# Sample attention of a hybrid decoder step: even and odd cache rows in the two column halves, and TensorE's order pinned by phases

## The chip, the cores and the metric

One core of one Trainium2 chip runs the whole kernel. The metric is device time in microseconds of one execution, the median of several runs; smaller is better.

## What is computed

One decoder layer for 256 prompt tokens and for 64 sample tokens (8 sequences with 8 new tokens each). The part that matters here is the attention of the sample tokens. Each sequence has 1024 rows of a compressed cache (512 latent values and 64 rotary values per row), which lie in 8 pages named by a page table. 8 heads attend from each of the 8 new tokens to these 1024 rows and, causally, to the 8 new rows of their own sequence:

```python
def mla_sample_attention(q_lat, q_pe, ckv_new, kpe_new, cache_ckv_l, cache_kpe_l, page_table):
    ckv_past = cache_ckv_l[page_table].reshape(Bd, -1, KV_RANK)
    kpe_past = cache_kpe_l[page_table].reshape(Bd, -1, ROPE_DIM)
    s_past = einsum('bthc,bsc->bhts', q_lat, ckv_past) + einsum('bthr,bsr->bhts', q_pe, kpe_past)
    s_new = einsum('bthc,bsc->bhts', q_lat, ckv_new) + einsum('bthr,bsr->bhts', q_pe, kpe_new)
    s_new = where(causal, s_new, -inf)
    p = softmax(concatenate([s_past, s_new], axis=-1) * MLA_SCALE, axis=-1)
    return (einsum('bhts,bsc->bthc', p[..., :P], ckv_past)
            + einsum('bhts,bsc->bthc', p[..., P:], ckv_new))
```

All of it is in 32-bit floats.

## The kernel before

The kernel is written for a framework that orders the instructions of each engine itself, from the order of the program and its own estimate of times, and that places every wait. Weights stream through three buffers `raw` of 1 MB (pool `wraw`); ScalarE and VectorE split them into a high and a low part (`whi`, `wlo`, pool `whl`, three of each), and TensorE multiplies each block three times (`mm3`). PSUM has four banks named `acc` and four named `aux`.

The sample attention stands between two projections that are put into its neighbourhood on purpose: `early_proj(0)` ahead of it, together with the last scores and values of the prompt attention, and `early_proj(1)` behind it, into which `sample_tail` lays the rest of the last sequence. It loops over the 8 sequences b. For each:

- `gather` (L738) fetches the 1024 cache rows by three indirect DMAs on GpSimd's queue: the rotary rows `kraw`, and the latent rows in two halves of 1 MB, the first into `craw` (pool `sr`, 3 buffers), the second into a `raw` buffer. Partition p holds 8 consecutive rows.
- `past_scores` (L755) is called once for each half. TensorE turns four 128x128 blocks at a time into one bank of `aux` (`transpose`, L134); ScalarE and VectorE in turn copy the bank to `th`. The queries `qst` (64 columns: 8 heads by 8 tokens) are the weights and `th` the moving operand. The 64 columns fill one half of the array, so two matmuls are issued for the two halves: half 0 adds up latent blocks 0 and 2, half 1 blocks 1 and 3, of the same 512 cache rows. `fold` (L731) adds the two halves: ScalarE copies partitions 64 to 127 of the bank down, VectorE adds. The sum is written to `Ss`, 64 partitions by 1088 columns.
- `new_scores` (L786) does the same for the 64 new rows of all sequences, with a mask (`C_NEW`) that leaves the sequence's own.
- `softmax` (L794) works on `Ss`, 64 partitions by 1088 columns, with the division at its end.
- `turn` (L802) turns the probabilities (eight blocks of 64x128 and one of 64x64), `values` (L812) multiplies them with the cache rows (eight matmuls with 512 columns, even ones in half 0, odd ones in half 1) and with the new rows `ckvs`, and `latent` (L822) adds the two halves by a matmul with a folding matrix and turns the result to `olat`.

The work of sequence b - 1 (`turn`, `values`) and of b - 2 (`latent`) is put between the steps of sequence b by the table `at`. What order TensorE gets in the end is the framework's choice. A matmul in 32-bit floats is two instructions in the profile (two LDWEIGHTS and two MATMUL), a transpose is one.

Of the kernel before, what the change touches and what calls it, by code (L numbers as in the profile page):

```python
# [18 lines left out]
NP = 256  # L19
NB = 8  # L20
# [18 lines left out]
C_NEW, C_VM, C_PEXP, C_PR, C_SEL, C_END = 1408, 1920, 1924, 2052, 2053, 2181  # L39


def _consts():
# [23 lines left out]
    for b in range(NB):  # L66
        ok = (r[None, :] // NT == b) & (r[None, :] % NT <= r[:, None] % NT)
        c[:NS, C_NEW + b * NS:C_NEW + (b + 1) * NS] = np.where(ok, 0.0, -1e30)
# [14 lines left out]
def tile_hgrn2_mla_step(  # L83
# [45 lines left out]

    def mm(out, lhsT, rhs, start, stop):  # L130
        nc.tensor.matmul(out, lhsT=lhsT, rhs=rhs, start=start, stop=stop)  # L131

    def transpose(out, in_, k):
        nc.tensor.transpose(out=out, in_=in_, identity=ident[:k, :k])  # L134
# [588 lines left out]
    with pool("sr", 3) as sr, pool("sc", 2) as sc, pool("s1") as s1:  # L723
# [31 lines left out]
        def past_scores(b, hf, S, kraw, craw, at):  # L755
            psc = bank(acc)
            ths = []

            def scores(f):
                for g in range(2):  # L760
                    mm(psc[64 * g:64 * (g + 1)], qst[:, f + g, b], ths[f + g], f == 0, False)

            for f in range(RF):
                pt = bank()
                for j in range(4):
                    transpose(pt[:, j * P:(j + 1) * P], craw[:, j, f * P:(f + 1) * P], P)
                th = sc.tile([P, 512], F32, name="th", bufs=4)
                cp(f, th, pt)
                ths.append(th)
                if f == 2:  # L770
                    scores(0)
                if f in at:
                    at[f]()
            pt = bank()
            for j in range(2):
                transpose(pt[:, j * P:(j + 1) * P],
                          kraw[:, 4 * hf + 2 * j:4 * hf + 2 * j + 2].rearrange("p o c -> p (o c)"), P)
            kt = sc.tile([P, 2, P], F32, name="ktp")
            cp(hf, kt, pt[:, 0:256].rearrange("p (j s) -> p j s", j=2))
            scores(2)  # L780
            pv_ = psc.rearrange("p (j o s) -> p o j s", j=2, o=2)
            for g in range(2):
                mm(pv_[64 * g:64 * (g + 1), g], qst[:, 4 + g, b], kt, False, True)
            fold(S, psc, slice(hf * 512, (hf + 1) * 512), 512)

        def new_scores(b, S):  # L786
            psn = bank(acc)
            for f in range(RF):
                g = f % 2
                mm(psn[64 * g:64 * (g + 1), 0:NS], qst[:, f, b], ckvT[:, f, NP:N], f < 2, f == 3)  # L790
            mm(psn[0:64, 0:NS], qst[:, 4, b], kpeT[:, NP:N], False, True)
            fold(S, psn, slice(PAST, PAST + NS), NS, cst[0:NS, C_NEW + b * NS:C_NEW + (b + 1) * NS])

        def softmax(S):  # L794
            mx = sc.tile([NS, 2], F32, name="mxs")
            nc.vector.tensor_reduce(out=mx[:, 0:1], in_=S, axis=AX.X, op=ALU.max)
            nc.vector.tensor_scalar(out=mx[:, 0:1], in0=mx[:, 0:1], scalar1=-SCALE, scalar2=None, op0=ALU.mult)
            nc.scalar.activation(out=S, in_=S, func=AF.Exp, scale=SCALE, bias=mx[:, 0:1], accum_out=mx[:, 1:2])
            nc.vector.reciprocal(out=mx[:, 1:2], in_=mx[:, 1:2])
            nc.vector.tensor_scalar(out=S, in0=S, scalar1=mx[:, 1:2], scalar2=None, op0=ALU.mult)  # L800

        def turn(S):  # L802
            pt, pt2 = bank(), bank()
            for j in range(8):
                transpose(pt[:, j * 64:(j + 1) * 64], S[:, j * P:(j + 1) * P], 64)
            transpose(pt2[0:64, 0:64], S[:, PAST:PAST + NS], 64)
            PT = sc.tile([P, 9, 64], F32, name="PTs")
            nc.scalar.copy(out=PT[:, 0:8], in_=pt.rearrange("p (j t) -> p j t", j=8))
            nc.vector.tensor_copy(out=PT[0:64, 8], in_=pt2[0:64, 0:64])
            return PT  # L810

        def values(PT, craws):  # L812
            po = bank(acc)
            for j in range(8):
                g = j % 2
                mm(po[64 * g:64 * (g + 1)], PT[:, j], craws[j // 4][:, j % 4], j < 2, j == 7)
            mm(po[0:64], PT[0:64, 8], ckvs, False, True)
# [586 lines left out]
```

## Time and profile before

| | us |
|---|---|
| median of 3 runs | 2173.68 (2171.99 to 2177.36) |
| the profiled execution, its own time | 2173.57 |
| its span, first to last instruction | 2171.5 |
| TensorE busy in the span | 2120.1 (98%) |
| VectorE busy | 1079.2 (50%) |
| ScalarE busy | 878.0 (40%) |
| GpSimd busy | 168.0 (8%) |

TensorE is busy almost all the time; the other engines work beside it. The mean granted TensorE clock is 0.993 of full speed. The sample attention lies between about 362 and 524 us of the span. Matmuls overlap, so their busy times add up to more than the time that they take; where the cost of a matmul is wanted, the distance between the starts of two weight loads (engine PEld) tells more.

### The profile page before, as it was taken

The page shows a single profiled execution, that of the slowest core. Times are in us where ns is not written, and L with a number is a line of the kernel's source. Part 1 is how long each engine was busy: PE and PEld are TensorE (multiplying, and loading weights), DVE is VectorE, ACT ScalarE, POOL GpSimd, SP SyncE. Part 2 cuts the span into 40 slices and gives each one's busy share as a digit, 9 for nine tenths or more (in the row PEclk, how much of TensorE's full clock was granted, in tenths as well). Part 3 has the DMA queues.
Part 4 walks back from the last instruction along what each step waited for, and adds up shares of the span by engine and source line. Part 5 has one row for each costly group of instructions (what it writes and reads, how often), then busy time and mean ns, then how long its engine had stood idle before and what let it go on. Part 6 is the DMA issues. An engine that isn't in the chain of part 4 may idle for free.

```text
span 2171.5 us, 34878 instructions
## 1 busy us (share of the span) xinstructions
PE 2120.1 (98%) x14716; PEld 1907.7 (88%) x14716; DVE 1079.2 (50%) x1648; ACT 878.0 (40%) x1328; POOL 168.0 (8%) x166
## 2 busy tenths in 40 slices
PE   6999999999999999999999899999999999999997
PEld 4788988457788889999999599999999999999996
DVE  3556754444865655533443643444444444444455
ACT  4332443334554444333343543434343333333353
POOL 0000001110432211000011000000000000000001
PEclk9999999999999999999999999999999999999998
DMA  8886455335567777766764555544444454454442
GB/s 255 319 301 238 152 190 197 111 128 160 185 215 240 232 241 253 241 208 204 252 213 141 196 177 168 173 144 148 155 150 144 153 155 142 150 156 148 145 151 71
DMA packets 327572, 401.94 MB, mean 185 GB/s; under 512 B 10985, under 2 KB 265529, under 8 KB 324473
## 3 DMA queue, kind: packets, MB, share of 16 engines
q1 hardware_dynamic: 301576, 363.07, 51.8%
q0 software_dynamic: 3584, 21.50, 2.8%
q10 hardware_dynamic: 22256, 15.16, 2.3%
q8 instruction: 115, 1.88, 0.4%
q14 instruction: 41, 0.33, 0.0%
HBM read 387.69 MB, written 12.01 MB: 184 GB/s over the span
## 4 chain that ended last, share of the span: by engine, by line
PE 92%; DVE 4%; ACT 1%; DMA 1%; issue 1%; POOL 0%; SPq 0%; DVEq 0%; ACTq 0%; POOLq 0%
PE acc L131 79%; PE aux L131 8%; PE aux L134 5%; DMA raw<-in_w_in_dram 1%; DVE wlo L143 1%; ACT whi L146 1%; DVE zu L1367 0%; DVE x L1284 0%; DVE X L143 0%; POOL qt L137 0%; DMA xt<-in_x_prompt_dram 0%; DVE zg L137 0%; DVE qn L494 0%; DVE bb L917 0%; POOL X L137 0%
## 5 line engine op out<-in xcount | busy, mean ns | idle before, releaser
L143 DVE TENSOR_TENSOR wlo<-raw,whi 128x1024 fp32r<-128x1024 f32 (+1 forms) x493 | 602.9, 1228 | 714.3 <-ACT whi L146 709.1
L146 ACT CAST whi<-raw 128x1024 fp32r<-128x1024 f32 (+1 forms) x493 | 502.1, 1025 | 807.6 <-PE acc L131 653.7
L131 PE MATMUL acc<-hh,whi 128*128 128x320 f32 x1168 | 369.8, 317 | 3.7 <-ACT hh L146 2.3
L131 PE MATMUL acc<-hl,whi 128*128 128x320 f32 x1168 | 362.6, 311 | 0.3 <-DVE hl L143 0.3
L131 PE MATMUL acc<-hh,wlo 128*128 128x320 f32 x1168 | 361.5, 311 | 0.0
L131 PE MATMUL acc<-uh,whi 128*128 128x320 f32 x1024 | 316.7, 309 | 0.0
L131 PE MATMUL acc<-gh,whi 128*128 128x320 f32 x1024 | 316.2, 309 | 0.0
L131 PE MATMUL acc<-gh,wlo 128*128 128x320 f32 x1024 | 316.1, 309 | 0.0
L131 PE MATMUL acc<-ul,whi 128*128 128x320 f32 x1024 | 316.1, 309 | 0.0
L131 PE MATMUL acc<-uh,wlo 128*128 128x320 f32 x1024 | 316.1, 309 | 0.0
L131 PE MATMUL acc<-gl,whi 128*128 128x320 f32 x1024 | 315.9, 309 | 0.0
L131 PEld LDWEIGHTS acc<-hh,whi 128*128 128x128 f32 x1168 | 220.2, 189 | 34.2 <-issue 17.5
L131 PEld LDWEIGHTS acc<-hl,whi 128*128 128x128 f32 x1168 | 220.5, 189 | 2.9 <-DVE hl L143 1.4
L131 PEld LDWEIGHTS acc<-hh,wlo 128*128 128x128 f32 x1168 | 219.6, 189 | 3.1 <-DVE wlo L143 2.5
L131 PEld LDWEIGHTS acc<-uh,whi 128*128 128x128 f32 x1024 | 192.5, 188 | 1.7 <-ACT u L1336 0.8
L131 PEld LDWEIGHTS acc<-gh,whi 128*128 128x128 f32 x1024 | 191.9, 187 | 1.8 <-ACT u L1337 0.8
L131 PEld LDWEIGHTS acc<-ul,whi 128*128 128x128 f32 x1024 | 192.4, 188 | 0.0
L131 PEld LDWEIGHTS acc<-uh,wlo 128*128 128x128 f32 x1024 | 192.4, 188 | 0.0
L131 PEld LDWEIGHTS acc<-gh,wlo 128*128 128x128 f32 x1024 | 192.0, 187 | 0.1
L131 PEld LDWEIGHTS acc<-gl,whi 128*128 128x128 f32 x1024 | 192.0, 188 | 0.0
L131 PE MATMUL aux<-raw,cT 128*32 128x512 f32 (+1 forms) x832 | 113.7, 593 | 16.1 <-DVE tt L137 11.2
L140 POOL TENSOR_TENSOR ssum<-ssum,sqt 128x320 f32<-128x320 f32 x26 | 25.9, 997 | 981.2 <-ACT sqt L1217 980.3
(411 smaller groups left out, 2602.7 us busy)
## 6 DMA issues: line engine op xcount, KB each, us to landing
raw<-in_w_ada_dram SPq DMA_DIRECT2D x96, 1024.0 KB, 6.9
raw<-in_w_up_dram SPq DMA_DIRECT2D x64, 1024.0 KB, 5.7
raw<-in_w_down_dram SPq DMA_DIRECT2D x64, 1024.0 KB, 5.8
raw<-in_w_in_dram SPq DMA_DIRECT2D x60, 1024.0 KB, 5.8
raw<-in_w_o_dram SPq DMA_DIRECT2D x16, 1024.0 KB, 5.8
raw<-in_w_in_dram SPq DMA_DIRECT2D x20, 512.0 KB, 6.4
raw<-in_w_b_out_dram SPq DMA_DIRECT2D x8, 1024.0 KB, 6.2
raw<-in_w_a_out_dram SPq DMA_DIRECT2D x8, 1024.0 KB, 5.8
```

The costliest lines, as they stand in the source:

```text
L131: nc.tensor.matmul(out, lhsT=lhsT, rhs=rhs, start=start, stop=stop)
L134: nc.tensor.transpose(out=out, in_=in_, identity=ident[:k, :k])
L140: (eng or nc.vector).tensor_tensor(out=out, in0=a, in1=b, op=ALU.add)
L143: return (eng or nc.vector).tensor_tensor(out=out, in0=a, in1=b, op=ALU.subtract)
L146: nc.scalar.copy(out=hi, in_=src)
```

## The change

The two column halves no longer split the latent blocks of the same rows; half 0 holds the even cache rows of a sequence and half 1 the odd ones. All 1024 scores of a sequence then stand in one bank of 128 partitions by 512 columns, with nothing to fold.

- `turn_keys` turns one latent block of all 1024 rows into two banks (g = 0: even, g = 1: odd) and copies them to the two halves of one buffer from the pool `whl`, which the attention did not use before. `turn_rotary` turns the rotary rows into one bank, which serves both halves. `scores` multiplies; a sequence now has 10 matmuls with 512 columns (five pairs).
- `softmax` reads the bank itself: VectorE takes the maximum over 512 columns on 128 partitions, `swapped` exchanges the halves of a column, and the exponential goes from the bank to `Ss` with the sum beside it. The division is put off: the reciprocal `wgt` is applied as ScalarE copies the values' result from its bank.
- `turn` turns four blocks of 128x128; `values` has the eight matmuls with the cache rows alone.
- The scores of the new tokens (`new_scores`) are made once ahead of the loop, each sequence against its own 8 rows (40 matmuls with 8 columns). Their exponentials `pnew` are kept. In `sample_tail` they are scaled, turned once, spread over a block structure (`pown`, 64 by 512), multiplied with `ckvs` in four matmuls of 512 columns, and added to `olat`.
- `behind` puts every TensorE instruction of a `with` block behind the last one before it. Each sequence has four phases: three latent blocks turned, and `latent` of b - 2; scores of blocks 0 and 1; `turn` of b - 1, block 3 and the rotary rows turned; `values` of b - 1 and the scores of blocks 2, 3 and rotary.
- Pool `sr` has 5 buffers in place of 3, and three of eight half gathers go into `raw` in place of four. Constants shrink by 496 columns.

```diff
+    pe_last = [None]
+    def behind():
+        return tc.issue_after(pe_last[0].ins)
...
-        def fold(S, psc, cs, n, mask=None):
-            S2 = s1.tile([NS, 512], F32, name="Ss2")
-            nc.scalar.copy(out=S2[:, 0:n], in_=psc[64:P, 0:n])
-            if mask is not None:
-                add(S2[:, 0:n], S2[:, 0:n], mask)
-            add(S[:, cs], psc[0:64, 0:n], S2[:, 0:n])
...
-                if hf:
+                if (2 * b + hf) % 8 in (1, 3, 5):
                     craw = wraw.tile([P, 2048], F32, name="raw").rearrange("p (j c) -> p j c", c=RANK)
...
+        def new_scores():
+            psn = bank(acc)
+            for b in range(NB):
+                us, vs = slice(b * NT, (b + 1) * NT), slice(NP + b * NT, NP + (b + 1) * NT)
+                for f in range(RF):
+                    mm(psn[0:NS, us], qst[:, f, b], ckvT[:, f, vs], f == 0, False)
+                mm(psn[0:NS, us], qst[:, 4, b], kpeT[:, vs], False, True)
...
+        def turn_keys(ths, craws, f):
+            pair = whl.tile([P, 1024], F32, name="wlo" if f % 2 else "whi")
+            for g in range(2):
+                pt = bank()
+                for j in range(4):
+                    transpose(pt[:, j * P:(j + 1) * P], craws[j // 2][:, 2 * j % 4 + g, f * P:(f + 1) * P], P)
+                th = pair[:, 512 * g:512 * (g + 1)]
+                cp(f + g, th, pt)
+                ths[f, g] = th
...
+        def scores(b, psc, ths, f):
             for g in range(2):
+                mm(psc[64 * g:64 * (g + 1)], qst[:, f if f < RF else RF + g, b], ths.pop((f, g)), f == 0, f == RF)
...
+        def softmax(b, psc):
+            mx = sc.tile([P, 6], F32, name="mxs")
+            nc.vector.tensor_reduce(out=mx[:, 0:1], in_=psc, axis=AX.X, op=ALU.max)
+            swapped(mx[:, 1:2], mx[:, 0:1])
...
+            nc.scalar.activation(out=S, in_=psc, func=AF.Exp, scale=SCALE, bias=mx[:, 2:3], accum_out=mx[:, 3:4])
+            nc.scalar.activation(out=pnew[:, b], in_=snew[:, b], func=AF.Exp, scale=SCALE, bias=mx[0:NS, 2:3],
+                                 accum_out=lnew[0:NS, b:b + 1])
...
+            nc.vector.reciprocal(out=wgt[:, b:b + 1], in_=mx[:, 5:6])
...
-            mm(po[0:64], PT[0:64, 8], ckvs, False, True)
...
+            nc.scalar.activation(out=ot, in_=po, func=AF.Copy, scale=wgt[:, b:b + 1])
...
         for b in range(NB):
             kraw, craws = gather(b)
+            ths, psc = {}, bank(acc)
+            for f in range(3):
+                turn_keys(ths, craws, f)
+            if done:
+                latent(b - 2, done)
+            with behind():
+                scores(b, psc, ths, 0)
+                scores(b, psc, ths, 1)
+            with behind():
+                if prev:
+                    PT = turn(prev[0])
+                turn_keys(ths, craws, 3)
+                turn_rotary(ths, kraw)
+            with behind():
+                if prev:
+                    done = values(b - 1, PT, prev[1])
+                for f in range(2, 5):
+                    scores(b, psc, ths, f)
+                S = softmax(b, psc)
+            prev = S, craws
...
+            for f in range(RF):
+                pn = bank()
+                mm(pn, ckvs[:, f * P:(f + 1) * P], pown.rearrange("s b q -> s (b q)"), True, True)
+                ov = olat[:, f].rearrange("p h (b t) -> p b h t", t=NT)
+                add(ov, ov, pn.rearrange("p (b h t) -> p b h t", b=NB, h=NH))
```

How the change moves the instructions shows at three places. The first is TensorE's queue in the middle of the loop, before: twelve rows of about twenty-five that make one sequence (`th` are turned keys, `qst` queries, `PTs` turned probabilities; "x4" is four instructions of the program in a row).

```order
L134 MATMUL aux<-ident,Ss 128x64 x8
L134 MATMUL aux<-ident,Ss 64x64
L131 MATMUL acc<-th,qst 64x512
L134 MATMUL aux<-ident,raw 128x128 x4
L131 MATMUL acc<-th,qst 64x512
L134 MATMUL aux<-ident,raw 128x128 x4
L131 MATMUL acc<-craw,PTs 64x512 x4
L131 MATMUL acc<-raw,PTs 64x512 x4
L131 MATMUL acc<-ckvs,PTs 64x512
L134 MATMUL aux<-ident,kraw 128x128 x2
L131 MATMUL acc<-th,qst 64x512 x2
L131 MATMUL acc<-ktp,qst 64x2x128 x2
```

The same queue now, one whole sequence (a sequence whose two halves both lie in `craw`; the keys are now named `whi` and `wlo`):

```order
L139 MATMUL aux<-ident,craw 128x128 x24
L136 MATMUL aux<-cst,ot 128x64 x4
L136 MATMUL acc<-whi,qst 64x512 x2
L136 MATMUL acc<-wlo,qst 64x512 x2
L139 MATMUL aux<-ident,Ss 128x128 x4
L139 MATMUL aux<-ident,craw 128x128 x8
L139 MATMUL aux<-ident,kraw 128x128 x4
L136 MATMUL acc<-craw,PTs 64x512 x4
L136 MATMUL acc<-raw,PTs 64x512 x4
L136 MATMUL acc<-whi,qst 64x512 x2
L136 MATMUL acc<-wlo,qst 64x512 x2
L136 MATMUL acc<-ktp,qst 64x512 x2
```

The matmuls on half the columns stood in six places of a sequence, some alone; now they stand in two blocks of two and seven pairs. The second place is VectorE's queue around a softmax, before:

```order
L140 TENSOR_TENSOR Ss<-acc,Ss_4268 64x512
L727 COPY th<-aux 128x512
L796 TENSOR_REDUCE mxs<-Ss 64x1
L826 COPY olat<-aux 128x32x8
L797 TENSOR_SCALAR mxs<-mxs 64x1
L727 COPY th<-aux 128x512
L799 RECIPROCAL mxs<-mxs 64x1
L800 TENSOR_SCALAR Ss<-Ss,mxs 64x1088
```

And now:

```order
L804 TENSOR_REDUCE mxs<-acc 128x1
L798 COPY mxs<-mxs 64x1
L799 COPY mxs<-mxs 64x1
L732 COPY whi<-aux 128x512
L806 SCALAR_TENSOR_TENSOR mxs<-mxs,mnew 128x1
L732 COPY wlo<-aux 128x512
L808 TENSOR_SCALAR mxs<-mxs 128x1
L732 COPY whi<-aux 128x512
L840 COPY olat<-aux 128x32x8
L145 TENSOR_TENSOR mxs<-mxs,lnew 128x1
```

The wide additions and the wide scaling are gone, and small steps stand between the three key copies of the next sequence. The third place is TensorE's queue ahead of the loop, before (`Sp`, `PTp` and `vv` belong to the last prompt heads):

```order
L134 MATMUL aux<-ident,Sp 128x128 x3
L131 MATMUL aux<-PTp,vv 128x128 x3
L134 MATMUL aux<-ident,Sp 128x128 x3
L131 MATMUL aux<-PTp,vv 128x128 x3
L134 MATMUL aux<-ident,craw 128x128 x12
```

And now, around the second transposes of `Sp`:

```order
L136 MATMUL acc<-ckvT,qst 64x8 x4
L136 MATMUL acc<-kpeT,qst 64x8
L136 MATMUL acc<-ckvT,qst 64x8 x3
L136 MATMUL aux<-PTp,vv 128x128 x3
L139 MATMUL aux<-ident,Sp 128x128 x3
L136 MATMUL acc<-ckvT,qst 64x8
L136 MATMUL acc<-kpeT,qst 64x8
```

Before, the transposes of `Sp` and the matmuls on `PTp` followed each other directly, and the first `craw` came behind them; now 23 and 17 of the 40 small matmuls stand in between.

## Rows read from the trace of the kernel before

**Rows 1.** The page's chain that ended last, shares of the span by engine.

```profile
PE 92%; DVE 4%; ACT 1%; DMA 1%; issue 1%; POOL 0%; SPq 0%; DVEq 0%; ACTq 0%; POOLq 0%
```

**Rows 2.** Windows: loop middle, start, tail; us, busy per engine (instructions), clock, DMA share, GB/s.

```profile
395.67:501.18 105.51, 105.51 (x631) 54.08 (x631) 47.16 (x93) 41.57 (x75) 13.19 (x14) 1.00 0.39 131
362.06:395.67 33.61, 30.91 (x178) 15.98 (x176) 11.56 (x23) 11.10 (x22) 2.19 (x3) 1.00 0.28 105
501.18:524.47 23.29, 23.29 (x150) 18.35 (x150) 7.83 (x13) 6.67 (x10) 0.00 (x0) 1.00 0.48 136
```

**Rows 3.** Timeline of weight loads, one sequence: start us, us, instruction, idle before.

```profile
415.18 0.86 PEld L134 LDWEIGHTS aux<-ident,craw 128*128 128x128 f32 x8 [0.38 <-issue]
416.00 0.97 PEld L131 LDWEIGHTS aux<-cst,ot 128*128 128x128 f32 x8
416.84 0.48 PEld L134 LDWEIGHTS aux<-ident,craw 128*128 128x128 f32 x4
417.49 0.20 PEld L131 LDWEIGHTS acc<-th,qst 128*64 128x64 f32 x4 [0.17 <-issue]
418.50 0.42 PEld L134 LDWEIGHTS aux<-ident,craw 128*128 128x128 f32 x4 [0.81 <-issue]
...
419.30 0.19 PEld L131 LDWEIGHTS acc<-th,qst 128*64 128x64 f32 x2 [0.17 <-issue]
...
421.60 0.86 PEld L134 LDWEIGHTS aux<-ident,raw 128*128 128x128 f32 x8
422.62 0.60 PEld L134 LDWEIGHTS aux<-ident,Ss 64*128 64x128 f32 x9 [0.17 <-issue]
423.32 0.19 PEld L131 LDWEIGHTS acc<-th,qst 128*64 128x64 f32 x2
424.32 0.42 PEld L134 LDWEIGHTS aux<-ident,raw 128*128 128x128 f32 x4 [0.81 <-DVE Ss L140]
...
426.49 0.20 PEld L131 LDWEIGHTS acc<-craw,PTs 128*64 128x64 f32 x4 [0.17 <-issue]
...
430.08 0.19 PEld L131 LDWEIGHTS acc<-ckvs,PTs 64*64 64x64 f32 x2 [0.81 <-issue]
431.08 0.20 PEld L134 LDWEIGHTS aux<-ident,kraw 128*128 128x128 f32 x2 [0.81 <-issue]
```

**Rows 4.** The same view at the start: the last prompt head, the first cache rows.

```profile
364.53 0.74 PEld L131 LDWEIGHTS aux<-PTp,vv 128*128 128x128 f32 x6 [2.07 <-ACT PTp L692]
...
366.36 0.74 PEld L131 LDWEIGHTS aux<-PTp,vv 128*128 128x128 f32 x6 [0.80 <-ACT PTp L692]
367.02 1.34 PEld L134 LDWEIGHTS aux<-ident,craw 128*128 128x128 f32 x12
```

**Rows 5.** The same view further on: small matmuls on half the columns in a row.

```profile
536.38 0.70 PEld L131 LDWEIGHTS aux<-part,kT 128*64 128x64 f32 x15
```

**Rows 6.** The same view: first of 24 projection matmuls, and what follows them.

```profile
520.99 0.19 PEld L131 LDWEIGHTS acc<-hh,whi 128*128 128x128 f32 x1
...
524.47 7.26 PEld L131 LDWEIGHTS aux<-olat,raw 128*128 128x128 f32 x64
```

**Rows 7.** Groups by line and form, 362 to 524 us: busy us, mean ns, idle before.

```profile
L727 DVE COPY th<-aux 128x512 f32<-128x512 f32 x32 | 21.8, 682 | 22.9 <-PE aux L134 22.8
...
L729 ACT COPY th<-aux 128x512 f32<-128x512 f32 x32 | 18.7, 586 | 17.0 <-PE aux L134 16.6
...
L796 DVE TENSOR_REDUCE mxs<-Ss 64x1 f32<-64x1088 f32 x8 | 10.2, 1269 | 0.0
...
L798 ACT ACTIVATE Ss<-Ss,mxs 64x1088 f32<-64x1088 f32 x8 | 9.6, 1202 | 3.2 <-DVE mxs L797 3.2
```

**Rows 8.** DMA issues, 330 to 540 us: the first halves' gathers, us to landing.

```profile
craw<-in_cache_ckv_dram,pidx POOLq DMA_INDIRECT x8, 8.3
```

**Rows 9.** TensorE's timeline and a window (columns as in rows 2) behind the attention.

```profile
567.21 0.64 PE L134 MATMUL aux<-ident,rp 128*96 128x128 f32 x4 [1.83 <-DVE rp L965]
569.00:572.00 3.00, 3.00 (x16) 2.55 (x12) 2.94 (x6) 1.55 (x4) 0.00 (x0) 0.50 0.01 3
```

More of the change, by code (lines that the diff above doesn't have):

```diff
@@ L65, in _consts @@
     r = np.arange(NS)
-    for b in range(NB):
-        ok = (r[None, :] // NT == b) & (r[None, :] % NT <= r[:, None] % NT)
-        c[:NS, C_NEW + b * NS:C_NEW + (b + 1) * NS] = np.where(ok, 0.0, -1e30)
+    c[:NS, C_NEW:C_NEW + NT] = np.where(np.arange(NT)[None, :] <= r[:, None] % NT, 0.0, -1e30)
+    c[:NS, C_OWN:C_OWN + NB] = r[:, None] // NT == np.arange(NB)[None, :]
     for b in range(4):
@@ L128, in log_exp_tables @@
             nc.scalar.preload_act_table_set("natural_log_exp_and_others")
+    pe_last = [None]
+    def behind():
+        return tc.issue_after(pe_last[0].ins)
     def mm(out, lhsT, rhs, start, stop):
-        nc.tensor.matmul(out, lhsT=lhsT, rhs=rhs, start=start, stop=stop)
+        pe_last[0] = nc.tensor.matmul(out, lhsT=lhsT, rhs=rhs, start=start, stop=stop)
     def transpose(out, in_, k):
-        nc.tensor.transpose(out=out, in_=in_, identity=ident[:k, :k])
+        pe_last[0] = nc.tensor.transpose(out=out, in_=in_, identity=ident[:k, :k])
     def mul(out, a, b, eng=None):
@@ L753, in gather @@
             return kraw, craws
[L755 to L763, printed above, removed]
+        snew = s1.tile([NS, NB, NT], F32, name="snew")
+        pnew = s1.tile([NS, NB, NT], F32, name="pnew")
+        mnew = s1.tile([P, NB], F32, name="mnew")
+        lnew = s1.tile([P, NB], F32, name="lnew")
@@ L784, in past_scores @@
[L784 to L800, printed above, removed]
@@ L802, in turn @@
-        def turn(S):
[L803 to L809, printed above, removed]
+                    transpose(pt[:, j * P:(j + 1) * P], craws[j // 2][:, 2 * j % 4 + g, f * P:(f + 1) * P], P)
@@ L810, in turn, with values @@
+        def turn(S):
+            pt = bank()
+            for j in range(4):
+                transpose(pt[:, j * P:(j + 1) * P], S[:, j * P:(j + 1) * P], P)
+            PT = sc.tile([P, 4, 2, 64], F32, name="PTs")
+            nc.scalar.copy(out=PT, in_=pt.rearrange("p (j g t) -> p j g t", j=4, g=2))
             return PT
-        def values(PT, craws):
+        def values(b, PT, craws):
             po = bank(acc)
-            for j in range(8):
-                g = j % 2
-                mm(po[64 * g:64 * (g + 1)], PT[:, j], craws[j // 4][:, j % 4], j < 2, j == 7)
-            mm(po[0:64], PT[0:64, 8], ckvs, False, True)
+            for j in range(4):
+                for g in range(2):
+                    mm(po[64 * g:64 * (g + 1)], PT[:, j, g], craws[j // 2][:, 2 * j % 4 + g], j == 0, j == 3)
@@ L818, in values @@
             ot = s1.tile([P, RANK], F32, name="ot")
-            nc.scalar.copy(out=ot, in_=po)
+            nc.scalar.activation(out=ot, in_=po, func=AF.Copy, scale=wgt[:, b:b + 1])
             return ot
@@ L827, in latent @@
                                   in_=pt[:, 0:256].rearrange("p (f h t) -> p f h t", f=4, h=NH))
[L829 to L838 removed]
+        new_scores()
+        prev, done = None, None
         for b in range(NB):
             kraw, craws = gather(b)
[L842 to L848 removed]
@@ L851, in sample_tail @@
+            with behind():
[5 more added lines that the diff above has]
+            prev = S, craws
         def sample_tail():
+            latent(NB - 2, done)
             PT = turn(prev[0])
             yield
-            ot = values(PT, prev[1])
+            ot = values(NB - 1, PT, prev[1])
+            mul(pnew, pnew, bc(wgt[0:NS, :, None], [NS, NB, NT]))
```

62 lines of the change are left out of this document (28 added, 34 removed).

## Prediction

> **What bounds the kernel now.** I read the chain that ended last, then windows of the stage, then the weight loads of one sequence. The chain runs over TensorE for 92% of the span [rows 1], so time is won only where TensorE's own queue gets shorter. The windows divide the stage, 362.06 to 524.47 us, which is 162.41 us long [rows 2]. Its middle, 105.51 us, holds six equal turns of the loop, 17.59 us each; in it TensorE is busy throughout at a granted clock of 1.00, while VectorE works 47.16 us and ScalarE 41.57 us, under half of it. So the loop costs what TensorE's queue costs, and the work of the other two engines is covered.
>
> What fills a turn is seen in the starts of the weight loads [rows 3]. Eight transposes take 0.82 us (415.18 to 416.00), so 0.105 us each, rounded up. `latent` takes 0.84 us. A pair of 512-column matmuls, one for each half, takes 1.01 us to the next transpose (417.49 to 418.50). Four pairs in a row take 3.59 us (426.49 to 430.08), so a further pair costs 0.86 us, and 0.15 us of the 1.01 is the way out of half-column work; the way in shows as 0.17 us idle. A lone matmul takes the same 1.00 us (423.32 to 424.32): its other half stands empty. The queue has two of these in every sequence. The matmul on `ckvs` takes 1.00 us as well (430.08 to 431.08).
>
> **The change, part by part.** Everything on TensorE, since the rest is covered.
>
> *One turn of the loop now.* 24 transposes 2.52; `latent` 0.84; way in 0.17; two pairs 1.01 + 0.86 = 1.87; 16 transposes (4 of `Ss`, 8, 4) 1.68; way in 0.17; seven pairs 1.01 + 6 x 0.86 = 6.17. Sum 13.42 us against 17.59, so 4.17 less. It comes from two lone matmuls that become a pair (0.86 and a way out), `ckvs` (1.00), the new tokens' five small matmuls (at most 0.86, below), four of six trips in and out of half-column work (4 x 0.32 = 1.28), and the rest in the changes to row halves. Six turns: 80.5 against 105.51.
>
> *The start.* Before, 33.61 us pass from 362.06 to the first of these turns [rows 2]. Of the first 4.96 (to the first `craw` at 367.02) TensorE waits 2.07 + 0.80 us for `PTp` [rows 4] and works 2.09. The 40 small matmuls, 80 instructions, are put into these waits. In this form they are not in the trace. Fifteen weight loads of 64 columns in a row take 0.70 us, 0.047 each [rows 5]; the block of 2.30 us that holds such matmuls (419.30 to 421.60) leaves, without its pair (0.86), half-length pair (0.43) and way out (0.15), 0.86 us for ten, 0.086 each [rows 3]. I take 0.06, nearer to the undisturbed row: 4.8 us (3.8 to 6.9). With four trips of 0.16 the start is 2.09 + 4.8 + 0.64 = 7.5 us. The first sequence has no `turn`, `values` or `latent`: 2.52 + 0.17 + 1.87 + 1.26 + 0.17 + 2.73 = 8.7. The second has no `latent`: 12.6. Together 28.8.
>
> *The end.* Before, 23.29 us [rows 2]. The 96 matmuls of `early_proj(1)` cost 3.48 us for 24 [rows 6], 13.9 in all, before and after. Now beside them: two `latent` 1.68, `turn` 0.42, `values` 3.59 + 0.17, one small transpose with its trip 0.4, and four matmuls on `ckvs`. These use half the rows and cannot pair; by the lone matmul each is 0.86, with a trip 3.75 us. Sum 10.0, with the projection 23.9.
>
> *Sum.* 28.8 + 80.5 + 23.9 = 133.2 us against 162.41: 29.2 less if TensorE never waits.
>
> *What waits remain.* Each turn still has copies ahead of matmuls, and the first turns start empty; I allow 0.25 us for each of the eight, 2.0 in all. Nothing in the trace prices these waits in the new order. The lower bound is none, as in the middle window where TensorE stands still nowhere; the upper bound is 1 us per turn, about one copy and the step that waits for it. Below none is excluded, since the sum already counts bare queue time. 29.2 - 2 is about 27 us.
>
> *What must stay covered.* VectorE per turn: five copies of 512 columns at 0.68 [rows 7], 3.4 us; the maximum from the bank, taken in proportion to 1269 ns for 1088 columns, 0.6; some nine small steps at up to 0.2, 1.8; `olat` 0.4. That is 6.2 of 13.4 us. ScalarE: three key copies and the copies to `PTs` and `ot` at 0.59, the exponential in proportion to 1202 ns 0.6, its sums and the small exponential 0.6: 4.2. Both have room in total. The tight place is in time: the maximum waits for the last pair, and its exponential stands behind three key copies in ScalarE's queue. Copies end some 3.1 us after the last pair, the exponential some 4.0; TensorE wants `Ss` after 24 transposes, `latent`, way in, two pairs: 5.4 us. The slack is 1.4 us. `PTs` is wanted 1.26 us after the four transposes of `Ss`, and a copy takes 0.59.
>
> Gathers: a half lands 8.3 us after issue [rows 8]. Eight half buffers now hold four sequences where six held three, and the rotary buffers free in the third phase of two turns earlier, more than a turn ahead of use. GpSimd's queue gains one memset far ahead and loses none of the 24 DMAs. A turn's 2.4 MB in 13.4 us is some 176 GB/s against 131 now, at a DMA share of 0.39. Three raw buffers free earlier, so SyncE's weight loads for `early_proj(1)` do not come later. The smaller constants are covered by the early projections. All of these at nothing; were a gather late, each turn would wait at most those 8.3 us.
>
> **The forecast.** The profiled execution took 2173.57 us, 2.07 more than its span; the median of the runs is 2173.68, so the two agree. 2173.6 - 27 gives **2146.6 us**. Its own range: 31.5 us saved with cheap small matmuls and no waits, 2142; 21 saved with a full microsecond of waits per turn and dear ones, 2152.5.
>
> **Rivals.**
>
> *The softmax and the copies set the pace.* Against it: slack of 1.4 us, engines half idle. For it: ScalarE's queue puts the exponential behind copies that themselves wait for four `aux` banks, and VectorE has small steps between its copies. If each of eight turns loses 2.5 us more than I allow, a third of the gain stays: 2146.6 + 20 = 2167. If it is 1.5 us: 2158.6. I take the latter as this rival's time. It decides from 3.4 us per turn (27 / 8), where nothing is left.
>
> *The gain is given back behind the stage.* The eight loads for the heads' values and the next projections come closer together. For it: the next stretch has its own waits (1.83 us in [rows 9]). Against it: the tail moves only 136 GB/s [rows 2]. At most one gather's time late, half of it on the path, 5 us: 2152.
>
> *TensorE's clock falls in the long runs of transposes; slower than before.* The row: behind the attention, after 1.83 us idle, the granted clock was 0.50 over 569 to 572 us, the lower of its two levels, 1.2 GHz [rows 9]. In the attention it is 1.00 in all three windows [rows 2], with runs of up to 17 transposes (421.60 to 423.32) [rows 3]; the change makes runs of 24. Were all transposes of the loop run at half clock, 316 of them at 0.105 us more, 33 us would be added: 2146.6 + 33 = 2180, slower. It decides where over 80% (27 / 33) of the transposes run slow. The Trainium skill, page "TensorE: Matmul & The Clock Gate", section "Part 4: PE-mode transpose", says that transposes do not count as TensorE activity for the clock as matmuls do; that rule speaks against longer runs of them. By that rule the sum would go the way of this rival; the trace does not bear it out, as a quarter of a turn is transposes at a full clock today.
>
> That the change would not do what it says can be left aside: the new queue shows whole pairs and the four phases in every turn.
>
> **Chances.** Forecast 0.84, softmax and copies 0.09, given back behind 0.04, clock 0.03. A difference under 0.3% (6.5 us) cannot be told from none in this kernel. Faster by more: the first three but for 0.01, 0.96. Within: 0.01. Slower: 0.03. The range takes in the forecast's own range and the second rival, and its upper end goes a little into the first: 2142 to 2155; about 0.12 is left out.
>
> **What would show it.** A loop turn of 13.4 to 13.7 us, from the 24 transposes of one sequence to those of the next, with weight loads idle only at two trips; 0.86 us between pairs; the small matmuls within the start at 0.06 us; the four matmuls on `ckvs` at 0.86. Waits of TensorE for `PTs`, `Ss`, `whi` or `wlo` over half a microsecond per turn would show the first rival, a clock under 1.00 in the stage the third. Wrong outright: a turn over 17 us, or pairs that take 1.7 us because the halves do not run beside each other.

## The result, and the profile after

The changed kernel took 2154.8 us (median of four runs, 2151.27 to 2156.85). The kernel before took 2172.84 us beside it. The ratio is 0.9912, with a 95% interval of 0.9891 to 0.9933. The change is faster by about 18 us; 27 were forecast, and 2154.8 lies just inside the range. The profiled execution took 2156.85 us (span 2154.7), so it is the slowest of the four, 10.3 us over the forecast.

The page's chain, shares of the span by engine. TensorE still carries it, though less than in [rows 1], and more of it is "issue":

```profile
PE 88%; issue 5%; DVE 3%; DMA 2%; ACT 1%; POOL 1%; SPq 0%; DVEq 0%; ACTq 0%; POOLq 0%
```

Windows of the stage, columns as in [rows 2] (length; busy us of TensorE, its weight loads, VectorE, ScalarE and GpSimd; granted clock; share and GB/s of the DMA): the start up to the first key transposes, the first sequence, the second, the six turns of the loop, the tail. Two stretches at a lower clock follow.

```profile
361.09:370.96 9.87, 9.87 (x101) 9.32 (x100) 1.02 (x4) 1.62 (x4) 1.25 (x2) 0.71 0.98 404
370.96:382.01 11.05, 11.05 (x58) 7.38 (x57) 3.88 (x6) 2.35 (x4) 1.88 (x2) 0.80 0.10 28
382.01:395.27 13.26, 13.13 (x79) 6.67 (x77) 5.32 (x15) 4.58 (x10) 2.82 (x3) 1.00 0.50 164
395.27:479.60 84.33, 83.75 (x507) 45.62 (x505) 36.55 (x99) 30.42 (x63) 9.42 (x10) 1.00 0.41 136
479.60:503.53 23.93, 23.93 (x142) 18.86 (x141) 11.68 (x25) 5.47 (x10) 0.00 (x0) 1.00 0.50 152
365.18:375.42 10.24, 10.24 (x65) 9.88 (x64) 2.83 (x7) 1.65 (x3) 0.00 (x0) 0.50 0.60 240
1198.03:1218.51 20.48, 18.56 (x74) 7.96 (x70) 12.34 (x42) 10.22 (x20) 1.40 (x4) 0.50 0.63 233
```

The stage takes 142.44 us where it took 162.41 [rows 2]; 135.2 were forecast. The tail came out as forecast (23.93 for 23.9). The six turns take 14.05 us each for 13.42 and the allowance of 0.25. The start and the first sequence are 2.4 and 2.35 us over, and there the clock column shows something new: 0.71 and 0.80. From 365.18 to 375.42 us the granted clock was 0.50, the lower level, where the stage before ran at 1.00 throughout [rows 2]. A second stretch at 0.50, from 1198.03 to 1218.51 us, lies far behind the stage.

One turn in the timeline of weight loads (start us, us, instruction; in brackets the idle time before it and what ended it, "issue" being nothing that the profile shows), to be held against [rows 3]:

```profile
423.45 0.20 PEld L139 LDWEIGHTS aux<-ident,craw 128*128 128x128 f32 x2 [0.81 <-issue]
...
424.78 0.20 PEld L139 LDWEIGHTS aux<-ident,craw 128*128 128x128 f32 x2
424.95 0.25 PEld L139 LDWEIGHTS aux<-ident,raw 128*128 128x128 f32 x2
425.38 0.20 PEld L139 LDWEIGHTS aux<-ident,craw 128*128 128x128 f32 x2 [0.18 <-DVE whi L732]
425.55 0.25 PEld L139 LDWEIGHTS aux<-ident,raw 128*128 128x128 f32 x2
426.11 0.20 PEld L139 LDWEIGHTS aux<-ident,craw 128*128 128x128 f32 x2 [0.32 <-ACT wlo L734]
426.28 0.25 PEld L139 LDWEIGHTS aux<-ident,raw 128*128 128x128 f32 x2
426.50 0.97 PEld L136 LDWEIGHTS aux<-cst,ot 128*128 128x128 f32 x8
427.54 0.20 PEld L136 LDWEIGHTS acc<-whi,qst 128*64 128x64 f32 x4
...
429.41 0.42 PEld L139 LDWEIGHTS aux<-ident,Ss 128*128 128x128 f32 x4 [0.81 <-issue]
...
431.33 0.20 PEld L136 LDWEIGHTS acc<-craw,PTs 128*64 128x64 f32 x4 [0.17 <-issue]
...
437.49 0.20 PEld L139 LDWEIGHTS aux<-ident,craw 128*128 128x128 f32 x2 [0.81 <-issue]
```

The starts divide the turn: 24 key transposes 3.05 us, `latent` and the way in 1.04, two pairs 1.87, 16 transposes and the way in 1.92, seven pairs 6.16; in all 14.04. Four of these are the forecast's terms within 0.1 us. The first was to be 2.52 and is 0.53 over. Inside it the fifth bank of transposes (425.38) waits 0.18 us until VectorE has copied the second. The sixth (426.11) waits 0.32 us.

VectorE's queue at that place, in the timeline, and one row of ScalarE's: the maximum and the two swap copies stand ahead of VectorE's first key copy.

```profile
423.57 0.69 DVE L804 TENSOR_REDUCE mxs<-acc 128x1 f32<-128x512 f32 x1 [5.48 <-PE acc L136]
424.30 0.15 DVE L798 COPY mxs<-mxs 64x1 f32<-64x1 f32 x1
424.46 0.15 DVE L799 COPY mxs<-mxs 64x1 f32<-64x1 f32 x1
424.64 0.69 DVE L732 COPY whi<-aux 128x512 f32<-128x512 f32 x1
...
425.37 0.69 DVE L732 COPY wlo<-aux 128x512 f32<-128x512 f32 x1
...
425.48 0.59 ACT L734 COPY wlo<-aux 128x512 f32<-128x512 f32 x1 [0.74 <-PE aux L139]
```

The row of the sixth bank names ScalarE's copy, that of the fourth bank, which ends at 426.07 us. VectorE's copy of the third ends at 426.06. The row alone does not tell which of the two the sixth bank needed; the experiment with the copies by half does.

### The profile page after: what moved, and what is told of

Read it like the earlier page. It is cut to its first block, busy times and chain, and to the rows that moved or that the text cites. A ratio compares the mean times of both kernels' runs of the same rounds, so it can differ in the third digit from the quotient of the medians.

```text
span 2154.7 us, 34719 instructions
## 1 busy us (share of the span) xinstructions
PE 2105.6 (98%) x14637; PEld 1906.8 (88%) x14637; DVE 1069.3 (50%) x1665; ACT 864.2 (40%) x1312; POOL 168.7 (8%) x167
## 4 chain that ended last, share of the span: by engine, by line
PE 88%; issue 5%; DVE 3%; DMA 2%; ACT 1%; POOL 1%; SPq 0%; DVEq 0%; ACTq 0%; POOLq 0%
PE acc L136 76%; PE aux L136 8%; PE aux L139 4%; DMA raw<-in_w_in_dram 1%; DVE wlo L148 1%; POOL X L142 1%; ACT whi L151 1%; DMA raw<-in_w_ada_dram 1%; DMA xt<-in_x_prompt_dram 0%; DVE zu L1395 0%; DVE X L148 0%; DVE zg L142 0%; POOL qt L142 0%; ACT X L964 0%; DVE qn L499 0%
```

## The experiments

Times are read stage by stage from the traces, since the totals of one kernel spread by some 5 to 10 us. Turns and stages below are taken between first starts on TensorE; in this reading the changed kernel's turn is 14.04 us and its stage (first transposes of `Sp` to the first matmul on `olat`) 142.45. "Ratio" is against the kernel before in the same set of runs.

### The stretch at half clock: new scores left out, wide, in the loop

The stretch began 3.5 us after the first of the narrow instructions (8 moving columns), so these were the suspects.

```diff
-            psn = bank(acc)
...
-                for f in range(RF):
-                    mm(psn[0:NS, us], qst[:, f, b], ckvT[:, f, vs], f == 0, False)
-                mm(psn[0:NS, us], qst[:, 4, b], kpeT[:, vs], False, True)
...
+            nc.vector.tensor_copy(out=snew, in_=bc(cst[0:NS, None, C_NEW:C_NEW + NT], [NS, NB, NT]))
```

> The 80 narrow TensorE instructions of the new tokens' scores are left out (the scores are set to the mask alone), so nothing of them is computed; all else stands. Theory A: the run of these narrow instructions is what the TensorE clock falls after. Then the granted clock is 1.00 from 361 us to the end of the stage, the first key transposes wait only for the gather that was issued at 356.7 us and landed 8.7 us later, about 365.4 us instead of 371.0, the first sequence takes 8.7 to 9.0 us instead of 11.05, and the stage is about 7.7 us shorter, 134.7 us. Rival B: the clock falls because of the thin work at the stage's start as a whole (transposes, trips between layouts). Then a stretch at 0.50 stays near 365 us, the first sequence still takes about 11 us, and only the 80 instructions' own 0.058 to 0.107 us go, 4.6 to 6.3 us at most.

Measured: the clock still fell, from 367.4 to 370.8 us. The stage took 138.19 us, 4.3 less. The first key transposes began at 369.19 us, not at 365.4, because TensorE now waits there. Its timeline:

```profile
362.54 0.49 PE L139 MATMUL aux<-ident,Sp 128*128 128x128 f32 x3
365.92 0.94 PE L136 MATMUL aux<-PTp,vv 128*128 128x128 f32 x6 [2.89 <-ACT PTp L697]
366.69 0.49 PE L139 MATMUL aux<-ident,Sp 128*128 128x128 f32 x3
367.75 1.65 PE L136 MATMUL aux<-PTp,vv 128*128 128x128 f32 x6 [0.57 <-ACT PTp L697]
```

Without the narrow instructions TensorE stands still for 3.46 us until `PTp` is copied, the counterpart of the 2.07 and 0.80 us in [rows 4] (3.13 and 0.81 us in that view, of weight loads). So the narrow instructions, which take 6.5 us in the changed kernel's trace, lengthen the start by only 2.3 to 3.3 us: up to the first key transposes this run takes 6.65 us, the changed kernel's two traces 8.91 and 9.94. Theory A falls: the clock goes down without them too. Ratio 0.9882 (0.9852 to 0.9913).

```diff
-                us, vs = slice(b * NT, (b + 1) * NT), slice(NP + b * NT, NP + (b + 1) * NT)
+                us = slice(b * NS, (b + 1) * NS)
                 for f in range(RF):
-                    mm(psn[0:NS, us], qst[:, f, b], ckvT[:, f, vs], f == 0, False)
+                    mm(psn[0:NS, us], qst[:, f, b], ckvT[:, f, NP:N], f == 0, False)
```

> The same 80 instructions with 64 moving columns each in place of 8 (all new tokens, as in the kernel before), of which the own 8 are then taken. Theory A: the clock stays at 1.00; the second 34 of them, the values behind them and the first 24 key transposes run at full speed, 4 to 5 us less, and the wider instructions give back between 0 (if the weight load of 0.06 us sets their pace) and 4 us (if they take 0.11 us each, as transposes of 128 columns do). Stage between 137.5 and 142 us. Rival B: the clock falls as before near 365 us, and the stage takes 142.4 us or more.

Measured: a stretch at 0.50 from 369.3 us, 3.4 us long; from `Sp` to the first key transposes 11.33 us for 9.94, the first sequence 9.24 for 10.85, the stage 142.24. What the shorter stretch gave, the wider instructions took. As the stretch also changes its length with no edit at all (10.2 and 6.8 us, below), this run alone does not tell why it was shorter. Ratio 0.9882 (0.9857 to 0.9907).

```diff
-        new_scores()
...
                     done = values(b - 1, PT, prev[1])
+                new_scores(b)
                 for f in range(2, 5):
```

> The new tokens' scores of one sequence are made in that sequence's turn, between values and the last three score blocks, ten narrow instructions at a time among instructions of 512 columns. Theory A: no stretch at 0.50 in the stage; the start shortens by 5.5 us (first key transposes at about 365.4 us, as the gather lands), the first sequence by 2.2 us, and each of eight turns grows by 0.6 us, 4.7 us: stage about 139.4 us, 3 us less than now. Rival B: the clock falls near 365 us all the same, and the stage is no shorter than 142 us.

Measured: every turn is 0.57 us longer (14.61), as expected. The clock fell all the same, from 367.0 to 370.4 us, after waits of 2.90 and 0.57 us for `PTp`, with no narrow instruction ahead of it. The stage took 142.80 us, no gain: what the loop pays, 8 x 0.57 = 4.6 us, is more than the start gets back. The new scores are well placed where they are. In each of these three runs the stretch was 3.4 us long, and in none of the ten traces with the narrow instructions in place was it under 6.8; so they may lengthen it, though they are not what brings it about. One trace of each edit does not settle that. Ratio 0.9891 (0.9871 to 0.9911).

### The same kernel again, and the phases undone

> The changed kernel itself once more, beside the other kernels of this set, to see what moves without any edit. Theory: the stage is the same piece by piece (turn 14.04 us, stage 142 to 143 us), while the two stretches at half clock, near 365 us and near 1198 us, may come out with other lengths (so far 3.4 to 10.2 us and 10.2 to 23.9 us), and with them the total by several us. Rival: both stretches repeat at 10.2 and 20.5 us, so they belong to this kernel's order of work and not to the run.

Measured: turns of 14.03 to 14.04 us, the stage 140.87. The stretch in the start was 6.8 us long instead of 10.2, the later one 3.4 us instead of 20.5, and the profiled run took 2149.18 us instead of 2156.85. How much that later stretch costs is read from the first matmul on `bh` ahead of it and the first on `uh` behind it. In the kernel before, the changed kernel, and the changed kernel again:

```profile
873.87 0.41 PE L131 MATMUL acc<-bh,whi 128*128 128x320 f32 x1
...
1299.27 0.41 PE L131 MATMUL acc<-uh,whi 128*128 128x320 f32 x1
```

```profile
851.88 0.41 PE L136 MATMUL acc<-bh,whi 128*128 128x320 f32 x1
...
1282.65 0.41 PE L136 MATMUL acc<-uh,whi 128*128 128x320 f32 x1
```

```profile
849.74 0.41 PE L136 MATMUL acc<-bh,whi 128*128 128x320 f32 x1
...
1274.99 0.41 PE L136 MATMUL acc<-uh,whi 128*128 128x320 f32 x1
```

That is 425.40, 430.77 and 425.25 us. So 5.4 us of the profiled run's shortfall arose here, where the change touches nothing, and do not come back in the second trace. The kernel before has such a stretch at the same place too, 6.8 us long in its trace. Over all fourteen traces this way takes 425.2 to 426.9 us where its time at half clock is 10.2 us or less, and 430.6 to 431.8 where it is 13.7 us or more. The two go together; which brings the other is not shown. Ratio 0.9913 (0.9892 to 0.9934), as the first time.

```diff
     def behind():
-        return tc.issue_after(pe_last[0].ins)
+        return ExitStack()
```

> The pinning of TensorE's order alone is undone: column halves, softmax from the bank and the separate new tokens stay. The order then differs in one place of a turn: one of the two matmuls of the first score block goes ahead of the last four key transposes, alone. Theory: it runs without its partner (0.43 us more for the pair) and adds two trips between layouts of 0.15 to 0.17 us each, 0.75 us a turn, of which up to 0.3 us falls into the wait for a bank: a turn of 14.5 to 14.8 us, stage 3.5 to 6 us longer. Rival: it only fills the wait for the banks, and a turn stays within 0.1 us of 14.04 us; then the phases are worth nothing.

Measured: a turn of 14.88 us, 0.84 more, and a stage of 146.86. The timeline of weight loads shows the lone matmul among the transposes, 1.00 us from its start to the next, the same as the lone one of [rows 3]:

```profile
431.13 0.19 PEld L136 LDWEIGHTS acc<-whi,qst 128*64 128x64 f32 x2 [0.17 <-issue]
432.13 0.20 PEld L139 LDWEIGHTS aux<-ident,craw 128*128 128x128 f32 x2 [0.81 <-ACT whi L734]
```

It stands where the sixth bank's wait was, and costs this all the same. The pinning alone is worth 0.84 us a turn. Ratio 0.9921 (0.9900 to 0.9943).

### The wait in the first phase: copies, a borrowed bank, and who held the fourth

```diff
-                cp(f + g, th, pt)
+                cp(g, th, pt)
```

> ScalarE copies the key bank of the even rows and VectorE that of the odd rows in each column block, so that ScalarE has the first, third and fifth bank of a turn and no two banks in a row wait for VectorE. Theory: the 0.5 to 0.6 us that a turn is over 13.4 us is TensorE waiting for banks behind VectorE, which does the maximum (0.69 us) and two swap copies (0.15 us each) ahead of its first two key copies. Then the first 24 transposes of a turn take 2.6 to 2.7 us instead of 3.05, a turn 13.6 to 13.7 us, and the stage is 2.5 to 3.5 us shorter. Rival: the number of banks, not the split, sets it: the wait moves to ScalarE's third copy, and the turn stays within 0.1 us of 14.04. The start of the stage, with its clock, stays as it is in either case.

Measured: a turn of 13.82 us, the stage 139.83. The wait ahead of the sixth bank went, the one for VectorE ahead of the fifth (0.18 us) stayed. The edit moves the third bank's copy from VectorE to ScalarE, where it ends early (424.10 us, before the transposes of the sixth bank), and the fourth's to VectorE, where it ends late (424.74 us, after they began at 424.26): the sixth bank needed the third's copy, not the fourth's. So 0.22 us of the excess lies in the split of the copies. Ratio 0.9890 (0.9871 to 0.9909).

```diff
-                pt = bank()
+                pt = bank(acc if (f, g) == (0, 0) else None)
```

> The first bank of key transposes of a turn is taken from the pool of accumulator banks, so five banks, not four, take the six of the first 24 transposes. Theory: TensorE waits in that phase because a bank comes free only when VectorE, late by its maximum and swaps, has copied it; with a fifth bank the fifth key bank does not wait, and the sixth waits for an earlier copy: the 24 transposes take 2.6 to 2.8 us instead of 3.16, a turn 13.5 to 13.7 us, the stage 2.5 to 4 us shorter. Rival: the copies' pace itself sets it, then the wait moves to the latents' bank or to the scores, and the turn stays above 13.9 us.

> The fifth bank and the copies by half together. Theory: the rest of the wait (the copies by half alone left 0.18 us before the fifth bank) goes, a turn of 13.45 to 13.55 us, which is the forecast's 13.42 us and 0.08 us for transposes at 0.108 us instead of 0.105; stage 3.5 to 4.5 us shorter than the changed kernel's. Rival: one of the two already takes all that there is, and the turn is no shorter than with the better of them alone.

Measured: 14.01 us with the borrowed bank alone, 13.82 with the copies by half as well, so the borrowed bank does next to nothing. The stages take 142.24 and 140.71 us, the ratios are 0.9906 (0.9888 to 0.9924) and 0.9923 (0.9897 to 0.9949). In the trace with the borrowed bank alone the same two rows wait as before, though the first transposes go to `acc`:

```profile
422.15 0.20 PEld L139 LDWEIGHTS aux<-ident,craw 128*128 128x128 f32 x2 [0.20 <-DVE whi L732]
...
422.86 0.20 PEld L139 LDWEIGHTS aux<-ident,craw 128*128 128x128 f32 x2 [0.30 <-ACT wlo L734]
```

With four banks the fifth set should take the bank that the first left. It waits for the copy of the second. Both runs thus spoke against the theory as it stood, and led to the question of how many banks go round. The answer stands ahead of the stage. `ada_gen` sums a row of the modulation in one `aux` bank over four steps of four matmuls, and copies the sum to `adarow` after the fourth. Between the pairs of heads six steps are issued: a row and a half. TensorE's and ScalarE's rows in the changed kernel's timeline:

```profile
327.07 1.93 PE L136 MATMUL aux<-raw,cT 128*32 128x512 f32 x16
...
520.38 1.05 PE L136 MATMUL aux<-raw,cT 128*32 128x512 f32 x2
...
538.30 0.59 ACT L330 COPY adarow<-aux 128x512 f32<-128x512 f32 x1 [4.06 <-PE aux L136]
```

The half row begun at 327 us is finished only behind the stage, and its bank is not read until 538 us. The whole stage runs on three `aux` banks. The waits agree: with three in turn the fifth set takes the bank of the second, and the sixth that of the third. The kernel before held a bank in the same way:

```profile
328.04 1.92 PE L131 MATMUL aux<-raw,cT 128*32 128x512 f32 x16
...
559.22 0.59 ACT L325 COPY adarow<-aux 128x512 f32<-128x512 f32 x1 [4.06 <-PE aux L131]
```

So the held bank could have been read before the change. The two steps were now moved behind the stage.

```diff
-            if i < NH // 2 - 1:
+            if i < NH // 2 - 2:
                 next(ada_steps)
                 next(ada_steps)
...
         finish_side()
+        next(ada_steps)
+        next(ada_steps)
```

> In the changed kernel a projection of the modulation (rows of w_ada) is left half done when the stage begins: two of the four steps of one row have been issued, and its partial sum holds one of the four aux banks through the whole stage, so the key transposes go round three. Here these two steps (two loads of 1 MB, eight matmuls) are issued behind the stage's tail, together with the row's other two, and the fourth bank is free; nothing else changes. Theory: three banks are why a turn waits 0.5 us in its first phase and why a bank borrowed for the first transposes did not help (the fifth still reused the second's bank). Then with four the first 24 transposes take 2.6 to 2.7 us, a turn 13.5 to 13.6 us, six turns and the second sequence 3 to 4 us less; the two steps cost behind the stage what they no longer cost ahead of it, so the total falls by about 3 us. Rival: the pace of the copies, VectorE late by its maximum and swaps, sets the wait whatever the banks; then the turn stays above 13.9 us.

> The free fourth bank and the copies by half together. Theory (three banks are the cause): the free bank alone takes all of the wait, and the copies by half add nothing: a turn of 13.5 to 13.6 us as with the free bank alone. Rival (the copies' pace): only this one comes to 13.5 us, and the free bank alone stays at 13.8 us or above.

Measured: 13.60 us a turn with the bank alone (13.66 in one turn), 13.53 with the copies as well. The first phase with both, in the timeline of weight loads, has no wait left and takes 2.57 us (423.45 to 426.02):

```profile
423.45 0.20 PEld L139 LDWEIGHTS aux<-ident,craw 128*128 128x128 f32 x2 [0.81 <-issue]
...
425.15 0.25 PEld L139 LDWEIGHTS aux<-ident,craw 128*128 128x128 f32 x2
...
425.59 0.25 PEld L139 LDWEIGHTS aux<-ident,craw 128*128 128x128 f32 x2
...
426.02 0.97 PEld L136 LDWEIGHTS aux<-cst,ot 128*128 128x128 f32 x8
```

The held bank is the cause of nearly all of the wait; the copies by half, worth 0.22 us with three banks, are worth 0.07 with four. Two other ways to free the bank (below) give the same turn of 13.53 us. The totals did not follow. The stages, 140.62 and 141.69 us, gain less than the turns: the moved row's transposes and matmuls now stand in the tail (0.53 and 1.86 us, 495.67 to 498.06 us in the first of the two), and in the second the stretch at half clock in the start was 10.2 us long. The ratios are 0.9926 (0.9907 to 0.9946) and 0.9912 (0.9894 to 0.9931), no better than the changed kernel's. From the first matmul on `olat` to the first on `bh` the changed kernel takes 348.2 us, these two 358.2 and 355.6. The clock fell there twice, as two windows of the first show:

```profile
506.20:516.40 10.20, 8.73 (x46) 5.14 (x44) 5.49 (x11) 4.95 (x8) 0.92 (x1) 0.50 0.93 286
533.50:540.30 6.80, 5.27 (x35) 5.15 (x36) 2.31 (x5) 3.63 (x4) 4.94 (x5) 0.50 0.01 2
```

In the changed kernel's two traces the clock does not fall between the stage and `bh`; here it is 0.50 for 17.0 us in the first run and 13.7 in the second, which at half speed costs up to 8.5 and 6.8 us. So most of the 10.0 and 7.4 us can be the clock. Whether the moved steps and their loads of 1 MB bring that about is not shown.

```diff
-            if i < NH // 2 - 1:
-                next(ada_steps)
+            for _ in range(2 if i < NH // 2 - 1 else 2):
                 next(ada_steps)
...
-                cp(f + g, th, pt)
+                cp(g, th, pt)
...
-            next(ada_steps)
+            next(ada_steps, None)
```

> The bank is freed the other way: the row's last two steps are issued ahead of the stage, behind the last pair of heads, and the copies by half are kept; a later place does two steps fewer. Theory: the turn is 13.5 to 13.6 us again, since the bank is free however it is freed; the start of the stage comes later by the two steps' work ahead of it (eight matmuls and two loads of 1 MB, by 2 to 6 us), and as much comes off later, so the total is within 2 us of the kernel in which the steps are put behind the stage. Rival: a turn above 13.8 us, so that not the bank but something else in the moved steps had helped.

Measured: the turn is 13.53 us again, so it is the bank and not where the steps went. The total is the worst of all: ratio 0.9967 (0.9953 to 0.9981), outside the 2 us expected. Its stage starts at 365.88 us and takes 140.09, and its stretches at half clock from the stage on (10.2 us in the start, 3.4 at 528, 6.8 at 624, 3.4 and 10.2 after 1207) add up to 34 us up to there, against 30.7 and 10.2 in the changed kernel's two traces. How much of its loss is the moved work and how much the clock was not separated.

So the sum was moved and the steps left where they are.

```diff
-            ps = bank()
+            ps = bank(abank[0])
...
+                abank[0] = acc if i == 2 else None
                 next(ada_steps)
                 next(ada_steps)
+                abank[0] = None
...
-                cp(f + g, th, pt)
+                cp(g, th, pt)
```

> The half-done row keeps its place in the program, but its partial sum goes to an accumulator bank, of which the stage leaves one free; the copies by half are kept. No step of the projection is moved. Theory: with four aux banks a turn is 13.53 us, as where the steps were moved (13.60 us without the copies by half), the stage 4 us shorter than the changed kernel's 141 to 142.5 us, and since no load is moved behind the stage the total keeps it: about 0.2 percentage points better against the kernel before than the changed kernel (0.989 against 0.991). Rival: the last pair of heads, which uses three accumulator banks at a time, now waits for one, and the stage starts 2 to 4 us later, so that the total does not change.

Measured: turns of 13.53 us, the stage 137.24 us, the shortest of the kernels that compute everything. It did not start later (360.55 us against 361.23 and 361.86 in the changed kernel's traces), so the rival falls. The median is 2150.8 us, the ratio 0.9884 (0.9863 to 0.9904) against 0.9912 and 0.9913 for the changed kernel. The stage is shorter by 3.6 to 5.2 us than in the changed kernel's two traces, 3.6 against the one whose stretch at half clock is as long as here (6.8 us); that the total is shorter by as much fits, but the intervals overlap. Against the copies by half alone (stage 139.83 us with a stretch of the same 6.8 us, ratio 0.9890) the bank gives 2.6 us of the stage and nothing that the totals show.

## Why the prediction came out as it did

The mechanism was right. TensorE's queue sets the stage, and a shorter queue shortened it. *One turn*: paired matmuls, trips and `latent` came to within 0.1 us of their terms. *The end*: 23.93 for 23.9, with 0.86 us for each `ckvs` matmul (497.39 to 498.25 in the trace). *What must stay covered*: right for the softmax; `Ss` and `PTs` were never waited for, and the transposes of `Ss` followed the two pairs at once.

The step that failed in the loop is *What waits remain*. I allowed 0.25 us for each turn, 2.0 in all; the first phase alone waits 0.5. The six turns and the second sequence are 4.5 us over their terms, 2.5 more than the 2.0 allowed. Transposes at 0.108 us for 0.105 are about 0.1 us of that in a turn; the rest is the wait. The first rival had named the place, copies that wait for four `aux` banks, but the number was wrong: three went round, because a half-done row held one. With the fourth bank a turn is 13.60 or 13.53 us, within 13.42 + 0.25. The pace of the copies, with the maximum ahead of them, was thus only the second cause: it makes the wait with three banks, and almost none with four.

The step that failed in *The start* is its silent assumption of a full clock. The narrow instructions cost what was taken: 46 of them from 361.65 to 364.43 us, 0.060 each. The excess of the start and the first sequence, 2.37 + 2.35 = 4.7 us, is what a stretch of 10.24 us at half speed costs, up to 5.1. The changed kernel's other trace agrees: with 3.4 us less at half clock the same two pieces take 19.35 us for 20.92. Eight of the narrow instructions at either speed, in the timeline of weight loads (0.46 us to the next row at first, 0.85 later):

```profile
361.65 0.54 PEld L136 LDWEIGHTS acc<-ckvT,qst 128*64 128x64 f32 x8 [0.17 <-issue]
...
366.38 0.97 PEld L136 LDWEIGHTS acc<-ckvT,qst 128*64 128x64 f32 x8
```

The third rival had the clock fall, but in the loop and by its transposes. That did not happen: the clock was 1.00 over the 84.33 us of the six turns, with 40 transposes in each. The Trainium skill, page "TensorE: Matmul & The Clock Gate", section "Part 4: PE-mode transpose", says that transposes do not count as activity of TensorE as matmuls do; in this kernel runs of 24 of them, with matmuls between the runs, left the clock at 1.00.

The second rival, gain given back behind the stage, came true in size (5.4 us in the profiled run) but not in its mechanism. Up to `bh` another 1.1 us were gained; the loss came 700 us further on, with a longer stretch at half clock, which varies between runs of one kernel.

Against the forecast of 2146.6 us, the profiled run's 10.3 us are therefore: 4.7 the clock at the start, 2.5 the banks beyond what was allowed, 5.4 the way with the later stretch, less 1.0 for a stage that began earlier, 1.1 between stage and `bh`, and 0.2 rounding and the span's end. The median is 8.2 us over.

That the median lies within 2142 to 2155 us is in part luck. The forecast's own range was added up wrongly: by its terms, cheap small matmuls (1.0 us less) without waits save 30.2 us, not 31.5, and dear ones (2.1 us more) with a full microsecond of waits per turn save 19.1, not 21. That is 2143.4 to 2154.5 us in place of 2142 to 2152.5, and 2154.8 lies above both; only the part of the range that reaches into the first rival takes it in. The clock, the largest item of the miss inside the stage, had no term in the sum, and the profiled run lies outside the range.

What stays open is why the clock falls at the start. In the one trace of the kernel before it does not, in spite of waits of 2.07 and 0.80 us [rows 4]; in all thirteen traces of the changed kernel and its variants it does, for 3.4 to 10.2 us. Leaving the narrow instructions out, widening them or moving them did not prevent it, though it was shortest in these three runs.

## What to carry to other kernels

Before costing a phase by the buffers of its pool, count which of them are held across it by work that was begun earlier and is finished later; here one open accumulation took one of four banks for some 200 us. Where such work is in the way, change where its sum lives before changing when it runs: with two steps moved the total was no shorter (ratios 0.9926, 0.9912 and 0.9967), while with the sum moved the stage was the shortest. Short instructions that fill an existing wait are cheaper where the wait is than inside a full loop.

## What the runs showed of the hardware that was not expected

The granted clock of a stretch is not a property of the kernel alone. Two traces of the same kernel, with turns equal to 0.01 us, had 10.2 and 6.8 us at 0.50 in the start of the stage, and 20.5 and 3.4 us near 1200 us; their profiled runs differ by 7.7 us. The kernel before spreads as well, from 2170.57 to 2182.2 us in the seventeen runs of one set. An edit worth 3 to 5 us in this kernel is read from its stage and not from the total.
